# Float32r products that walk their moving rows and their sums from the last column to the first

## The chip, the core and the metric

The kernel runs on one NeuronCore of one Trainium2 chip. TensorE multiplies: it holds a block of weights (128 rows by up to 128 columns) and streams the columns of a moving operand from SBUF through it, adding the results into a PSUM bank of 512 float32 values per partition. VectorE (DVE), ScalarE (ACT) and GpSimd (POOL) do elementwise work, and SyncE (SP) issues most of the DMAs. The metric is the device time of one execution in microseconds, smaller is better. The kernel before takes 1236.33 us, the median of three runs (1235.86 to 1240.36).

## The reference

Two decoder layers over 512 tokens of width 1024, in float32. The mixer of layer 0 is a grouped state-space layer, that of layer 1 attention with forget gates; each is followed by a gated feed-forward block with a short causal convolution. The products with full weight matrices carry most of the arithmetic:

```
for i in range(2):
    hn = rmsnorm(h) * g * (1 + scale) + shift
    m  = s5_mixer(hn) if i == 0 else fox_mixer(hn)     # w_in, w_glu, w_out: 1024 x 1024 / w_in: 1024 x 3088, w_out
    h  = h + gate * m
    hn = rmsnorm(h) * g2 * (1 + scale2) + shift2
    a, b = split(hn @ w_up)                            # 1024 x 5632
    a  = conv_b + sum_j shift_right(a, 2 - j) * conv_w[j]
    h  = h + gate2 * ((silu(a) * b) @ w_down)          # 2816 x 1024
return rmsnorm(h) * final_g
```

The shifts, scales and gates come from a product of silu(c) with a matrix of 1024 x 3072 for each of the four sub-layers.

## The kernel before

**Layout.** Activations lie transposed: features on the 128 partitions (8 tiles of 128 for width 1024), the 512 tokens along the free axis. A weight matrix is cut into tiles of 128 x 128; a tile is the stationary operand and 512 (or 256) tokens of an activation are the moving one. One group of products, over all k tiles of the contraction, fills one PSUM tile of 128 x 512 (or 128 x 256) float32.

**Three products for one.** The operands are float32r, a float32 of reduced precision that TensorE takes in one pass. To keep the accuracy, each operand is split into a high and a low part: ACT writes the high part (`put_parts`, L277) and VectorE the difference (L278). Then high x high, high x low and low x high are added into the same sums. `mms` (L290 to L296) issues these three for one k tile: L294 is the line of nearly every float32r product of the gate and output projections of layer 0, of the query, key and output projections of layer 1, and of the feed-forward blocks where they are computed plainly. `product` (L298) calls it for all tiles: a first part (`head`), in halves of 256 tokens or over all 512; a middle part over all 512 tokens; and a last part (`tail`), always in halves of 256, so that the next norm can begin on the first half.

**Quarters.** In the feed-forward's up projection most pairs of output tiles go through `quarters` (L510), which computes a product of 2 x 2 blocks with seven block products instead of eight. `times` (L546 to L553) issues one block product: 4 k tiles, three parts each, over 256 tokens, 84 products for a pair of tiles, all at L550. The sums are copied or added by ACT (L557) and VectorE (L518).

**The gate of layer 0.** The first four tiles of the gate projection are computed while the state-space part still runs, in `glu_head` (L1189 to L1200, products at L1198, over 512 tokens), first with the high and then with the low parts of the weights.

**What is not float32r or not touched.** The state-space input projection (L1139, L1169) uses plain float32 over 512 tokens. The attention's value projection (L1361) has the activations as stationary operand and 256 (or 272) columns of the weights as moving ones, in float32r; logits (L1470) and weighted values (L1520) are float32r as well.

**Order.** Apart from the start, which is scheduled by hand, the order within each engine follows the program with a few instructions held behind others. TensorE runs its products in that order; semaphores tie it to ACT and VectorE, which split weights ahead of it and empty its sums behind it. Weights are loaded by SP's queue, three raw tiles ahead, and the split parts have five buffers.

Of the kernel before, what the change touches and what calls it, by code (L numbers as in the profile page):

```python
# [19 lines left out]
KT = D // P  # L20
# [46 lines left out]
def part_of(pool, shape, name, tag, bufs, aside=0):  # L67

    _, n, w = shape
    t = pool.tile([P, ROOM if bufs == WB else n * w + P], F32R, name=name, tag=tag, bufs=bufs)  # L70
    return t[:, aside:aside + n * w].rearrange("p (n w) -> p n w", w=w)


class Trunk:
# [215 lines left out]
    def mms(self, o, wk, x, k, nk, cols):  # L290
        (hi, lo) = wk[k]
        xhi, xlo = x(k) if callable(x) else (t[:, k] for t in x)
        for n, (wt, xt) in enumerate(((hi, xhi), (hi, xlo), (lo, xhi))):
            self.last_mm = self.nc.tensor.matmul(  # L294
                o, wt, xt[:, cols], start=(k == 0 and n == 0), stop=(k == nk - 1 and n == 2),
            )  # L296

    def product(self, w, ms, nk, x, evac, head=0, tail=0, after=None, ticks=0, halves=HALVES, tail_pool=(), first=None, step=None):  # L298
# [211 lines left out]
    def quarters(self, pool, l, f, x, finish):  # L510

        nc = self.nc
        H, N = KT // 2, S // 2
        t1, t2 = HALVES
        a, b = (self.raw([P, KT, P], self.io["w_up"][l][2 * f + j]) for j in range(2))
        a11, a12, a21, a22 = a[:, :H], a[:, H:], b[:, :H], b[:, H:]
        c, d = (pool.tile([P, 2, H, P], F32, name="sums", bufs=2) for _ in range(2))
        sub = lambda o, u, v, op=ALU.subtract: nc.vector.tensor_tensor(o, u, v, op)  # L518
        w = {}
        copied = self.copied  # L520

        def parts(src, names, *where):
            hi, lo = (
                pool.tile([P, H * P + P], F32R, name=n, tag="e" + n)[:, ASIDE:ASIDE + H * P].rearrange("p (n w) -> p n w", w=P)
                if where else part_of(self.wpool, [P, len(names) * H, P], n, n, WB, ASIDE)
                for n in ("w_hi", "w_lo")
            )
            with self.behind(*copied):
                self.put_parts(hi, lo, src)
            for j, n in enumerate(names):  # L530
                w[n] = hi[:, j * H:(j + 1) * H], lo[:, j * H:(j + 1) * H]

        parts(a, ("a11", "a12"))
        sub(c[:, 0], a21, a22, ALU.add)
        sub(c[:, 1], c[:, 0], a11)
        parts(c.rearrange("p n k m -> p (n k) m"), ("s1", "s2"))
        sub(d[:, 1], a11, a21)
        sub(d[:, 0], a12, c[:, 1])
        parts(d.rearrange("p n k m -> p (n k) m"), ("s4", "s3"))
        parts(a22, ("a22",), pool)  # L540
        quarter = lambda k, t: tuple(v[:, k * H:(k + 1) * H, t] for v in x)
        xs = {"b11": quarter(0, t1), "b21": quarter(1, t1), "b22": quarter(1, t2)}
        for n, v in self.tx.items():
            xs[f"t{n}"] = v

        def times(o, wn, xn, first=True):  # L546
            (whi, wlo), (xhi, xlo) = w[wn], xs[xn]
            for k in range(H):
                for n, (wt, xt) in enumerate(((whi, xhi), (whi, xlo), (wlo, xhi))):
                    self.last_mm = nc.tensor.matmul(  # L550
                        o, wt[:, k], xt[:, k], start=(first and k == 0 and n == 0), stop=(k == H - 1 and n == 2),
                        skip_group_check=True,
                    )  # L553

        def copy(o, last=False):
            t = self.tmp.tile([P, N], F32, name="nm_h", bufs=4)
            a = nc.scalar.activation(t, o, AF.Copy)  # L557
            if last:
                self.copied = [a.ins]
            return t  # L560

        p1, p5 = (self.mm.tile([P, S], F32, name="mmp")[:, :N] for _ in range(2))
        p2, p4 = (self.aux.tile([P, S], F32, name="aux")[:, :N] for _ in range(2))
        oa, ob = (self.tmp.tile([P, S], F32, name="nm_t") for _ in range(2))
        times(p1, "a11", "b11")
        c1 = copy(p1)
        times(p5, "s1", "t1")
        c5 = copy(p5)
        times(p2, "a12", "b21")
        sub(oa[:, t1], p2, c1, ALU.add)  # L570
        times(p1, "s2", "t2", False)
        c2 = copy(p1, True)
        times(p5, "s4", "b22", False)
        sub(oa[:, t2], p5, c2, ALU.add)
        finish(2 * f, oa, slice(0, S))
        times(p4, "a22", "t4")
        c4 = copy(p4)
        times(p1, "s3", "t3", False)
        sub(ob[:, t2], p1, c5, ALU.add)
        sub(ob[:, t1], p1, c4)  # L580
        finish(2 * f + 1, ob, slice(0, S))
# [98 lines left out]
class Ew:  # L680
# [29 lines left out]
    def sub(self, a, b, out=None):  # L710
        return self.tt(a, b, ALU.subtract, out)
# [70 lines left out]
class S5(Trunk):  # L782
# [292 lines left out]
    def s5(self, i, nxt):  # L1075
# [5 lines left out]
        with ExitStack() as stack:  # L1081
# [7 lines left out]
            with ExitStack() as start:  # L1089
# [11 lines left out]
                with tc.manual_schedule(engines={ENG.PE, ENG.Activation, ENG.DVE, ENG.SP}):  # L1101
# [53 lines left out]
                    first = self.tmp.tile([P, L, B], F32, name="uf", tag="nm_t")  # L1155
# [22 lines left out]
            yhi = ylo = None  # L1178
            raw, hi, lo, gps = {}, {}, {}, {}
# [9 lines left out]
            def glu_head(k, part):  # L1189

                for m in range(HEAD):
                    if part and m not in lo:
                        lo[m] = part_of(self.wpool, [P, KT, P], "w_lo", "w_lo", WB)
                        with tc.issue_after(self.scanned):
                            nc.vector.tensor_tensor(lo[m], raw[m], hi[m].bitcast(F32), ALU.subtract)
                    wt = (hi, lo)[part][m][:, k]
                    for xt in (yhi, ylo) if part == 0 else (yhi,):
                        nc.tensor.matmul(  # L1198
                            gps[m], wt, xt[:, k], start=(k == 0 and part == 0 and xt is yhi), stop=(k == KT - 1 and part == 1)
                        )  # L1200

            ps = self.aux.tile([KT, P], F32, name="aux")
# [9 lines left out]
            for m in range(KT):  # L1212
# [22 lines left out]
                if m == KT - 2:  # L1235
                    yhi = self.act.tile([P, KT, S], F32R, name="a_hi")
# [6 lines left out]
            for k in range(KT - 1):  # L1243
                if k == KT - 2:
                    parts(k)
                glu_head(k, 0)
            for k in range(KT - 1):
                glu_head(k, 1)
# [4 lines left out]
            for p in range(2):  # L1253
                glu_head(KT - 1, p)
# [386 lines left out]
```

## Time and profile before

One execution on the chip was profiled. The table gives what matters of it; busy time is the time in which an engine had at least one instruction running.

| | us |
|---|---|
| median of the runs (lowest, highest) | 1236.33 (1235.86, 1240.36) |
| the profiled execution, its own time | 1233.09 |
| its span, first to last instruction | 1231.3 |
| TensorE products | 1200.5 |
| TensorE weight loads | 1031.2 |
| VectorE | 1009.0 |
| ScalarE | 606.3 |
| GpSimd | 82.7 |

How to read it: each instruction has a start and a length, and its line in the kernel. The ends of products on TensorE are modelled and products overlap, so the length that a row shows for one product is longer than the distance between the starts of two that follow each other; where a rate matters, starts are compared. The chain that ended last is followed back from the last instruction, at each step to the work that released it. In the names of groups, `mmp` and `aux` are the PSUM tiles, `a_hi` and `a_lo` the parts of the normed activations, `ghi` and `glo` those of the gated values, `zhi` and `zlo` those of the gate's output in layer 0, `v` those of the attention's output, `w_hi` and `w_lo` those of weights or of the block sums in `quarters`. An engine's idle time is put down to what ended it.

### The profile page before, as it was taken

How to read it: one execution, taken by the hardware profiler on the slowest of the kernel's cores; microseconds unless marked ns; L12 is line 12 of the kernel's file. 1: busy time of each engine (PE TensorE's matmuls, PEld its weight loads, DVE VectorE, ACT ScalarE, POOL GpSimd, SP SyncE). 2: the span in 40 equal slices, each digit the busy share in tenths (PEclk: the TensorE clock that was granted, in tenths of full speed). 3: DMA queues.
4: the chain of work that ended last, by engine and by line, in shares of the span. 5: the costliest groups of instructions: out<-in, count | busy, mean ns of one | idle time of the engine just before them, and what ended most of it. 6: DMA issues, size and time to landing. Idle time of an engine off the chain costs nothing.

```text
span 1231.3 us, 20566 instructions
## 1 busy us (share of the span) xinstructions
PE 1200.5 (97%) x7921; PEld 1031.2 (84%) x7921; DVE 1009.0 (82%) x1872; ACT 606.3 (49%) x1137; POOL 82.7 (7%) x143
## 2 busy tenths in 40 slices
PE   7999999999999999999999999999999999999997
PEld 2466678898989899889899887878989999999987
DVE  7988886779899988799687578876899887888865
ACT  3543465335544543445443565664366554545443
POOL 0000000100000000000000243430000000000000
PEclk9999999999999999999999999999999999999999
DMA  9776668530354544444445543432122332323231
GB/s 356 244 237 215 223 225 286 192 129 35 129 178 158 192 161 160 152 168 132 125 139 190 176 150 124 147 118 94 70 69 95 120 122 77 116 86 123 95 96 69
DMA packets 74385, 183.83 MB, mean 149 GB/s; under 512 B 23231, under 2 KB 25631, under 8 KB 73263
## 3 DMA queue, kind: packets, MB, share of 16 engines
q1 hardware_dynamic: 68239, 161.02, 38.4%
q0 software_dynamic: 5760, 20.97, 5.0%
q8 instruction: 62, 1.02, 0.3%
q10 hardware_dynamic: 288, 0.52, 0.1%
q14 instruction: 36, 0.29, 0.1%
HBM read 175.57 MB, written 6.92 MB: 148 GB/s over the span
## 4 chain that ended last, share of the span: by engine, by line
PE 75%; DVE 15%; DMA 4%; issue 3%; ACT 2%; POOL 0%; SPq 0%; DVEq 0%; ACTq 0%; POOLq 0%
PE mmp L294 32%; PE mmp L550 16%; PE aux L550 6%; DVE w_lo L278 5%; PE mmp L1169 4%; PE mmp L1361 2%; DMA rawd<-in_w_down 2%; PE aux L971 2%; PE mmp L1198 2%; PE aux L1060 1%; PE aux L1500 1%; PE mmp L205 1%; PE aux L1052 1%; DVE ada_raw L247 1%; PE mmp L1109 1%
## 5 line engine op out<-in xcount | busy, mean ns | idle before, releaser
L278 DVE TENSOR_TENSOR w_lo<-raw,w_hi 128x1024 fp32r<-128x1024 f32 (+4 forms) x173 | 183.3, 1065 | 35.4 <-ACT w_hi L277 34.8
L277 ACT ACTIVATE w_hi<-raw 128x1024 fp32r<-128x1024 f32 (+4 forms) x173 | 154.8, 905 | 101.5 <-PE mmp L294 53.1
L294 PE MATMUL mmp<-ghi,w_hi 128*128 128x512 f32 (+1 forms) x392 | 145.1, 370 | 0.0
L294 PE MATMUL mmp<-glo,w_hi 128*128 128x512 f32 (+1 forms) x392 | 144.8, 369 | 0.0
L294 PE MATMUL mmp<-ghi,w_lo 128*128 128x512 f32 (+1 forms) x392 | 144.5, 369 | 0.0
L294 PE MATMUL mmp<-a_hi,w_hi 128*128 128x512 f32 (+1 forms) x376 | 138.8, 372 | 1.5 <-ACT a_hi L433 1.5
L294 PE MATMUL mmp<-a_hi,w_lo 128*128 128x512 f32 (+1 forms) x376 | 136.6, 364 | 0.3 <-DVE w_lo L278 0.3
L294 PE MATMUL mmp<-a_lo,w_hi 128*128 128x512 f32 (+1 forms) x376 | 136.2, 363 | 0.0
L550 PE MATMUL mmp<-w_hi 128*128 128x256 f32 x396 | 111.4, 281 | 2.6 <-ACT nm_h L557 2.6
L550 PE MATMUL mmp<-w_hi,w_lo 128*128 128x256 f32 x396 | 111.1, 281 | 0.7 <-DVE w_lo L278 0.7
L550 PE MATMUL mmp<-w_lo,w_hi 128*128 128x256 f32 x396 | 111.1, 281 | 0.0
L557 ACT ACTIVATE nm_h<-mmp 128x256 f32<-128x256 f32 x99 | 37.9, 384 | 131.5 <-PE mmp L550 131.5
L278 DVE TENSOR_TENSOR w_lo<-sums,w_hi 128x1024 fp32r<-128x1024 f32 x74 | 90.1, 1219 | 0.3 <-ACT w_hi L277 0.2
L294 PEld LDWEIGHTS mmp<-ghi,w_lo 128*128 128x128 f32 x392 | 74.2, 189 | 12.7 <-DVE w_lo L278 0.4
L294 PEld LDWEIGHTS mmp<-glo,w_hi 128*128 128x128 f32 x392 | 74.5, 190 | 11.1
L277 ACT ACTIVATE w_hi<-sums 128x1024 fp32r<-128x1024 f32 x74 | 76.7, 1054 | 14.4 <-DVE sums L518 11.2
L294 PEld LDWEIGHTS mmp<-ghi,w_hi 128*128 128x128 f32 x392 | 74.2, 189 | 11.4
L294 PEld LDWEIGHTS mmp<-a_hi,w_hi 128*128 128x128 f32 x376 | 70.6, 189 | 13.8 <-issue 2.6
L294 PEld LDWEIGHTS mmp<-a_hi,w_lo 128*128 128x128 f32 x376 | 70.9, 189 | 12.3 <-DVE w_lo L278 1.3
L362 DVE SCALAR_TENSOR_TENSOR h<-mmp,par,h 128x512 f32<-128x512 f32 (+1 forms) x100 | 68.1, 683 | 15.3 <-PE mmp L294 15.0
L294 PEld LDWEIGHTS mmp<-a_lo,w_hi 128*128 128x128 f32 x376 | 71.1, 189 | 9.7
L550 PEld LDWEIGHTS mmp<-w_hi 128*128 128x128 f32 x396 | 74.3, 188 | 3.0 <-ACT nm_h L557 3.0
(317 smaller groups left out, 3092.6 us busy)
## 6 DMA issues: line engine op xcount, KB each, us to landing
raw<-in_w_up SPq DMA_DIRECT2D x88, 512.0 KB, 3.3
raw<-in_ada_w SPq DMA_DIRECT2D x40, 512.0 KB, 6.3
ada_raw<-in_ada_t POOLq DMA_DIRECT2D x40, 512.0 KB, 3.9
nf<-nfd SPq DMA_DIRECT2D x8, 1152.0 KB, 6.5
raw<-in_fox_qk SPq DMA_DIRECT2D x16, 512.0 KB, 3.6
raw<-in_w_down SPq DMA_DIRECT2D x24, 320.0 KB, 3.0
rawd<-in_w_down SPq DMA_DIRECT2D x24, 256.0 KB, 3.4
raw<-in_w_down SPq DMA_DIRECT2D x16, 384.0 KB, 3.3
```

The lines of the kernel that those rows point to most:

```text
L205: self.last_mm = nc.tensor.matmul(ps[32 * qq:32 * qq + 32, :], self.sc32[:, k, :], w[:, q * S:(q + 1) * S], start=(step is steps[0]), stop ...
L247: nc.vector.tensor_tensor_reduce(w, w, self.c_row, 1.0, 0.0, ALU.mult, ALU.add, sums[:, j:j + 1])
L277: nc.scalar.activation(hi, src, AF.Copy)
L278: return nc.vector.tensor_tensor(lo, src, hi.bitcast(F32), ALU.subtract)
L294: self.last_mm = self.nc.tensor.matmul(o, wt, xt[:, cols], start=(k == 0 and n == 0), stop=(k == nk - 1 and n == 2),)
L362: add = self.nc.vector.scalar_tensor_tensor(self.h[:, m, cols], ps, self.par[i][:, 16 + m:17 + m], self.h[:, m, cols], op0=ALU.mult, op1=A ...
L550: self.last_mm = nc.tensor.matmul(o, wt[:, k], xt[:, k], start=(first and k == 0 and n == 0), stop=(k == H - 1 and n == 2), skip_group_che ...
L557: a = nc.scalar.activation(t, o, AF.Copy)
L971: nc.tensor.matmul(ps[g2][:, j, cols], x[rows, a + j, r].rearrange("p c j -> p (c j)"), self.rr[rows, planes, q, :], start=(j == 0 and r = ...
L1169: nc.tensor.matmul(ps, w[m][:, k, :], x[:, k], start=(k == 0), stop=(k == KT - 1))
L1198: nc.tensor.matmul(gps[m], wt, xt[:, k], start=(k == 0 and part == 0 and xt is yhi), stop=(k == KT - 1 and part == 1))
L1361: self.last_mm = nc.tensor.matmul(ps[q, b][:, :n], xt[:, k, tb], wt, start=(k == 0 and i == 0), stop=(k == KT - 1 and i == 2),)
```

## The change

Three lines issue the same products with both patterns reversed. The moving operand is read from its last column to its first, and the sums are written from the last column of the PSUM tile to the first, so each column's sum lands where it did. The stationary operand, the order of the products, their number and their flags (which clears, which adds) stay as they were.

```diff
@@ mms @@
         for n, (wt, xt) in enumerate(((hi, xhi), (hi, xlo), (lo, xhi))):
             self.last_mm = self.nc.tensor.matmul(
-                o, wt, xt[:, cols], start=(k == 0 and n == 0), stop=(k == nk - 1 and n == 2),
+                o[:, ::-1], wt, xt[:, cols][:, ::-1], start=(k == 0 and n == 0), stop=(k == nk - 1 and n == 2),
             )
@@ quarters, times @@
                     self.last_mm = nc.tensor.matmul(
-                        o, wt[:, k], xt[:, k], start=(first and k == 0 and n == 0), stop=(k == H - 1 and n == 2),
+                        o[:, ::-1], wt[:, k], xt[:, k, ::-1], start=(first and k == 0 and n == 0), stop=(k == H - 1 and n == 2),
                         skip_group_check=True,
                     )
@@ s5, glu_head @@
                         nc.tensor.matmul(
-                            gps[m], wt, xt[:, k], start=(k == 0 and part == 0 and xt is yhi), stop=(k == KT - 1 and part == 1)
+                            gps[m][:, ::-1], wt, xt[:, k, ::-1], start=(k == 0 and part == 0 and xt is yhi), stop=(k == KT - 1 and part == 1)
                         )
```

## The prediction

> **What bounds the kernel now.** I read the totals first, then the chain of work that ended last, then TensorE's share line by line, then its start times one after another.
>
> ```profile
> span 1231.3 us, 20566 instructions
> ...
> PE 1200.5 (97%) x7921; PEld 1031.2 (84%) x7921; DVE 1009.0 (82%) x1872; ACT 606.3 (49%) x1137; POOL 82.7 (7%) x143
> ...
> PEclk9999999999999999999999999999999999999999
> ...
> PE 75%; DVE 15%; DMA 4%; issue 3%; ACT 2%; POOL 0%; SPq 0%; DVEq 0%; ACTq 0%; POOLq 0%
> ```
>
> TensorE (PE) is busy for 1200.5 us of a span of 1231.3 us, at a full granted clock in every slice; 75% of the chain is its work. VectorE, the next, has 18% of slack over the whole. So what one product costs on TensorE is what the kernel costs, and a saving on another engine would be worth little.
>
> The change touches three lines. Their rows for the whole span (length of the stretch, TensorE busy with the count of products, weight loads busy with their count):
>
> ```profile
> 0.00:1232.00 1232.00, 584.49 (x2808) 473.72 (x2808) 1.00 0.44 149
> ...
> 0.00:1232.00 1232.00, 332.68 (x2772) 330.71 (x2772) 1.00 0.44 149
> ...
> 0.00:1232.00 1232.00, 22.65 (x96) 17.80 (x96) 1.00 0.44 149
> ```
>
> These are L294, L550 and L1198: 5,676 products, 939.8 us of TensorE's 1200.5. Next, how many of them are 512 columns wide, from the groups kept apart by shape:
>
> ```profile
> L294 PE MATMUL mmp<-ghi,w_hi 128*128 128x512 f32 x312 | 121.8, 390 | 0.0
> L550 PE MATMUL mmp<-w_hi 128*128 128x256 f32 x396 | 111.4, 281 | 2.6 <-ACT nm_h L557 2.6
> ...
> L294 PE MATMUL mmp<-a_hi,w_hi 128*128 128x512 f32 x280 | 111.9, 400 | 0.0
> ...
> L294 PE MATMUL mmp<-v,w_hi 128*128 128x512 f32 x96 | 30.2, 396 | 1.1 <-DVE lo L278 1.1
> ...
> L294 PE MATMUL mmp<-v,w_lo 128*128 128x512 f32 x48 | 18.7, 390 | 0.0
> L294 PE MATMUL mmp<-zhi,w_hi 128*128 128x512 f32 x48 | 18.7, 389 | 0.0
> ...
> L294 PE MATMUL aux<-a_hi,w_hi 128*128 128x512 f32 x8 | 3.1, 389 | 0.0
> ```
>
> Each product comes in three parts of equal count (v's two high parts share one name, hence 96 and 48). So L294 has 3 x (312 + 280 + 48 + 8) + 96 + 48 = 2,088 products of 512 columns and 2,808 - 2,088 = 720 of 256. L1198 adds 96 of 512, and all of L550 (84 for each of 33 pairs of tiles) are of 256. Together: **2,184 products of 512 columns and 3,492 of 256.**
>
> The 389 and 281 ns of these rows are no cost: ends are modelled and products overlap. The cost is the distance of starts. From the order of time (start, length, work):
>
> ```profile
> 417.03 0.39 PE L294 MATMUL mmp<-a_hi,w_hi 128*128 128x512 f32 x1
> ...
> 427.91 0.39 PE L294 MATMUL mmp<-ghi,w_hi 128*128 128x512 f32 x1
> ...
> 433.35 0.28 PE L550 MATMUL mmp<-a_hi,w_hi 128*128 128x256 f32 x1
> ...
> 436.18 0.28 PE L550 MATMUL aux<-a_hi,w_hi 128*128 128x256 f32 x1
> ...
> 664.06 0.28 PE L1361 MATMUL mmp<-w_lo,a_hi 128*128 128x256 f32 x1
> ...
> 671.77 0.28 PE L1361 MATMUL mmp<-w_hi,a_hi 128*128 128x256 f32 x1
> ...
> 128.12 4.56 PE L1169 MATMUL mmp<-a_x,raw 128*128 128x512 f32 x10
> 132.61 0.64 PE L205 MATMUL mmp<-raw,s_sc 128*32 128x512 f32 x4
> ```
>
> Between the first two rows lie 48 starts: 10.88 us / 48 = 226.7 ns for 512 columns. Between the next two lie 24: 2.83 / 24 = 117.9 ns for 256. L1361, float32r too but not touched, has 68 starts in 7.71 us: 113.4 ns for 256, exactly half of 226.7. So the time of a float32r product is its streaming, 0.443 ns a column, and L550 pays 4.5 ns more a product on top. The last two rows give a third price: ten products of plain float32 and 512 columns take 4.49 us, 449 ns each, twice the streaming.
>
> **The change, part by part.** No instruction, DMA, wait or buffer is added, removed or moved. Each of the 5,676 products starts at its last column and steps by minus one, on the moving side and on the side of the sum; the same bytes are read and written, and weights are loaded as before. So all that can change is the time of one product. The profile shows no product with a negative step in its innermost run, so this is an unknown that has to be bounded.
>
> *Low end: nothing.* What other engines show of odd patterns (times are min/median/max):
>
> ```profile
> L1042 DVE TENSOR_TENSOR ua<-ua,ub x8: 684/688/692, 69.0 to 179.4; 128x512 f32<-128x512 f32 x8
> ...
> L1039 DVE TENSOR_TENSOR ua<-m,s_rot x8: 683/688/693, 67.4 to 178.0; 128x512 f32<-128x512 f32 x8
> ...
> L1171 ACT ACTIVATE uf<-mmp x7: 597/598/637, 48.2 to 150.0; 128x512 f32<-128x512 f32 x7
> ...
> L212 ACT ACTIVATE ada_rows<-mmp x4: 597/598/599, 22.4 to 167.6; 128x512 f32<-128x512 f32 x4
> ...
> L1186 ACT ACTIVATE a_hi<-yt x8: 1122/1177/1239, 150.4 to 191.2; 128x512 fp32r<-128x512 f32 x8
> ...
> L277 ACT ACTIVATE zhi<-nm_t x8: 630/634/637, 198.8 to 223.6; 128x512 fp32r<-128x512 f32 x8
> ```
>
> L1042 takes its two halves in reverse (an outer step of minus 256) and costs what L1039 costs, 688 ns. L1171 reads sums from PSUM at a step of 8 elements for the same 598 ns as L212's plain read. Only L1186, which writes SBUF at a step of 8, pays: 1177 against 634 ns. A walk backwards stays among neighbours, so these rows leave a price of nothing open. [...]
>
> ```profile
> L277 ACT ACTIVATE w_hi<-raw 128x1024 fp32r<-128x1024 f32 x97 | 101.9, 1056 | 68.5 <-PE mmp L294 43.5 <-PE mmp L1361 7.7 <-DMA raw<-in_w_up 7.6
> ...
> L277 ACT ACTIVATE w_hi<-raw 128x512 fp32r<-128x512 f32 x33 | 20.6, 625 | 11.4 <-DMA raw<-in_w_up 8.0 <-PE aux L550 2.9 <-ACT w_hi L277 0.5
> ```
>
> (1056 - 625) / 512 = 0.84 ns an element. TensorE takes a column in 0.443 ns, reading one 4-byte element per partition and adding another into PSUM: almost exactly two in ACT's time for one. [...]
>
> *High end.* [...] The nearest row of TensorE is L1169's: 449 ns for 512 columns. Farther up stands L1186's price, 1177 - 634 = 543 ns more for 512 elements.
>
> **I take the lost pair**, at the row of the same engine, shape and element size: 449 ns for 512 columns, half of it for 256. Sum: 2,184 x (449 - 226.7) ns = 485 us, plus 3,492 x (224.5 - 117.9) ns = 372 us: 857 us more. Some of it fills time in which TensorE now waits: 1231.3 - 1200.5 = 30.8 us of idle, and 584.5 - (2,088 x 0.2267 + 720 x 0.1179) = 26.3 us in L294 and 332.7 - 2,772 x 0.1179 = 5.9 us in L550 of products that follow one another late. Of these 63 us I give back 20, because part lies where nothing changes (before 168 us, and in the attention's own products) and part is the tail of a product ahead of a wait. VectorE's 1009 us and ACT's 606 us then lie well inside. The profiled execution's own time is 1233.1 us (span 1231.3 and 1.8 around it), 0.3% under the median of 1236.3 us; 1233 + 857 - 20 = **2,070 us**. Its own range: 2,010 us, if all 63 us are filled and L1169's 449 ns has some 2% of changes between groups in it, to 2,125 us, if nothing is filled and streaming doubles exactly (2,184 x 227 + 3,492 x 113 ns = 890 us).
>
> [...]
>
> **The rivals.**
> [...]
> *A smaller price.* The backward walk costs at its start only, for instance L550's 4.5 ns once more on each product (5,676 x 4.5 = 26 us, 1,260 us), or a quarter of the streaming (0.25 x (2,184 x 226.7 + 3,492 x 113.4 ns) = 223 us, 1,456 us). For it: L550's 4.5 ns show that something besides the columns counts. Against it: nothing in the trace makes it depend on direction.
> *Overlap lost.* A product waits until the one before has ended: the 389 and 281 ns of the groups instead of 226.7 and 117.9. That is 2,184 x 162 + 3,492 x 163 ns = 923 us, less 20: 2,136 us. The 256-column distance tells it from the lost pair, 281 against 225.
> *Every element by itself*, at L1186's price: 2,184 x 543 + 3,492 x 271 ns = 2,132 us more, about 3,350 us. Against it: L1186 steps by eight elements.
> *Faster.* L550's extra 4.5 ns go because weights and moving rows, read at the same time, then meet less often: (2,772 + 720) x 4.5 ns = 16 us, 1,217 us. For it: L1361 runs without them. Against it: nothing says that direction is the reason.
>
> **How the numbers follow.** Lost pair 0.46, no price 0.20, smaller price 0.13, overlap lost 0.06, every element 0.07, faster 0.08. Predicted: 2,070 us, the likeliest. The range of 1,230 to 2,140 us takes in lost pair, no price, smaller price and overlap lost, 0.85; it is wide because the two main cases lie 830 us apart. What a measurement of this kernel can tell from no change is about 0.5%. Faster 0.08, same 0.20, slower 0.72.
>
> **What the changed profile would show.** Right: starts of L294's 512-column products 430 to 455 ns apart, of L550's 215 to 232, while L1169 stays at 449 and L1361, whose products stay forward, at 113; VectorE's and ACT's busy times unchanged and their shares down to half and 30%; the chain over 85% TensorE; the granted clock full. A clock below full would spoil the comparison of distances. Wrong at the pair: distances of 227 and 118. Wrong at the overlap: 389 and 281. Wrong in what is given back: distances as said but a time outside 2,010 to 2,125 us. If only one of the two sides, reading or adding, is to blame, this one profile can't say which.

## The result, and the profile after

The changed kernel takes 1244.38 us, the median of 13 runs (1240.75 to 1252.66), against 1235.86 us of the kernel before (13 runs, 1230.60 to 1243.71). The ratio is 1.0078, with a 95% interval of 1.0057 to 1.0098: slower by 8.5 us by the two medians and by some 9.6 by the ratio, where 834 us more had been predicted. The way was right, the size was not.

The totals, the granted clock and the chain of waits of the kernel after (its profiled execution took 1242.51 us):

```profile
span 1240.7 us, 20613 instructions
...
PE 1214.0 (98%) x7921; PEld 1034.2 (83%) x7921; DVE 1007.4 (81%) x1872; ACT 606.2 (49%) x1137; POOL 82.6 (7%) x143
...
PEclk9999999999999999999999999999999999999999
...
PE 82%; DVE 11%; DMA 3%; ACT 2%; issue 2%; DVEq 0%; SPq 0%; ACTq 0%
```

The span grew by 1240.7 - 1231.3 = 9.4 us. TensorE's busy time grew by 1214.0 - 1200.5 = 13.5 us, and its idle time fell from 30.8 to 26.7 us, which gives 4.1 us back. VectorE and ACT work as long as before.

The three lines of the change, over the whole span (L294, L550, L1198; columns as in the prediction, and the third number from the end is the mean granted clock):

```profile
0.00:1242.00 1242.00, 596.92 (x2808) 475.47 (x2808) 0.99 0.45 148
...
0.00:1242.00 1242.00, 332.97 (x2772) 331.38 (x2772) 0.99 0.45 148
...
0.00:1242.00 1242.00, 23.19 (x96) 17.74 (x96) 0.99 0.45 148
```

L294 takes 12.4 us more and L1198 0.5; L550, all of 256 columns, 0.3. So the price sits in the products of 512 columns. The same products in order of time as those that the prediction showed (start, length, work):

```profile
419.42 0.40 PE L294 MATMUL mmp<-a_hi,w_hi 128*128 128x512 f32 x1
...
430.62 0.40 PE L294 MATMUL mmp<-ghi,w_hi 128*128 128x512 f32 x1
...
436.22 0.28 PE L550 MATMUL mmp<-a_hi,w_hi 128*128 128x256 f32 x1
...
439.05 0.28 PE L550 MATMUL aux<-a_hi,w_hi 128*128 128x256 f32 x1
...
670.02 0.28 PE L1361 MATMUL mmp<-w_lo,a_hi 128*128 128x256 f32 x1
...
677.73 0.28 PE L1361 MATMUL mmp<-w_hi,a_hi 128*128 128x256 f32 x1
```

The 48 starts of 512 columns now take 11.20 us instead of 10.88: 233.3 ns each, 6.7 more. The 24 of 256 columns take 2.83 us as before, 117.9 ns in the mean, though no longer evenly: by the starts in the trace they come 115, 118 and 120 ns apart in turns. L1361, which stayed forward, is at 113.4. From the distances, 2,184 x 6.67 ns = 14.6 us; L294 and L1198 show 13.0, because some late starts got shorter (by the trace, the time by which 512s start late fell from 6.6 to 3.9 us).

### The profile page after: what moved, and what is told of

It reads as the page before. It is cut to its first block, busy times and chain, and to the rows that moved or that the text cites. A ratio compares the mean times of both kernels' runs of the same rounds, so it can differ in the third digit from the quotient of the medians.

```text
span 1240.7 us, 20613 instructions
## 1 busy us (share of the span) xinstructions
PE 1214.0 (98%) x7921; PEld 1034.2 (83%) x7921; DVE 1007.4 (81%) x1872; ACT 606.2 (49%) x1137; POOL 82.6 (7%) x143
## 4 chain that ended last, share of the span: by engine, by line
PE 82%; DVE 11%; DMA 3%; ACT 2%; issue 2%; DVEq 0%; SPq 0%; ACTq 0%
PE mmp L294 39%; PE mmp L550 16%; PE aux L550 6%; PE mmp L1169 4%; DVE w_lo L278 3%; PE mmp L1361 2%; PE aux L971 2%; DMA rawd<-in_w_down 1%; PE aux L1500 1%; PE mmp L1198 1%; PE mmp L205 1%; PE aux L1060 1%; PE aux L1052 1%; PE mmp L1109 1%; PE aux L1470 1%
## 5 line engine op out<-in xcount | busy, mean ns | idle before, releaser
L294 PE MATMUL mmp<-ghi,w_hi 128*128 128x512 f32 (+1 forms) x392 | 147.9, 377 | 0.0
L294 PE MATMUL mmp<-glo,w_hi 128*128 128x512 f32 (+1 forms) x392 | 147.6, 376 | 0.0
L294 PE MATMUL mmp<-ghi,w_lo 128*128 128x512 f32 (+1 forms) x392 | 147.6, 376 | 0.0
L294 PE MATMUL mmp<-a_hi,w_hi 128*128 128x512 f32 (+1 forms) x376 | 140.7, 377 | 1.5 <-ACT a_hi L433 1.5
L294 PE MATMUL mmp<-a_hi,w_lo 128*128 128x512 f32 (+1 forms) x376 | 138.2, 368 | 0.0
L294 PE MATMUL mmp<-a_lo,w_hi 128*128 128x512 f32 (+1 forms) x376 | 138.2, 368 | 0.0
L550 PE MATMUL mmp<-w_hi 128*128 128x256 f32 x396 | 110.9, 280 | 1.7 <-ACT nm_h L557 1.7
L550 PE MATMUL mmp<-w_hi,w_lo 128*128 128x256 f32 x396 | 111.6, 282 | 0.5 <-DVE w_lo L278 0.5
L550 PE MATMUL mmp<-w_lo,w_hi 128*128 128x256 f32 x396 | 111.5, 282 | 0.0
L294 PEld LDWEIGHTS mmp<-ghi,w_lo 128*128 128x128 f32 x392 | 74.7, 191 | 14.1
L294 PEld LDWEIGHTS mmp<-glo,w_hi 128*128 128x128 f32 x392 | 74.9, 191 | 12.9
L294 PEld LDWEIGHTS mmp<-ghi,w_hi 128*128 128x128 f32 x392 | 74.8, 191 | 12.7
L294 PEld LDWEIGHTS mmp<-a_hi,w_hi 128*128 128x128 f32 x376 | 70.3, 188 | 15.2 <-issue 2.6
L294 PEld LDWEIGHTS mmp<-a_hi,w_lo 128*128 128x128 f32 x376 | 70.7, 188 | 12.8
L294 PEld LDWEIGHTS mmp<-a_lo,w_hi 128*128 128x128 f32 x376 | 70.8, 188 | 10.9
L550 PEld LDWEIGHTS mmp<-w_hi 128*128 128x128 f32 x396 | 74.4, 188 | 1.9 <-ACT nm_h L557 1.9
```

Of the source, the lines that this page charges most:

```text
L294: self.last_mm = self.nc.tensor.matmul(o[:, ::-1], wt, xt[:, cols][:, ::-1], start=(k == 0 and n == 0), stop=(k == nk - 1 and n == 2),)
L550: self.last_mm = nc.tensor.matmul(o[:, ::-1], wt[:, k], xt[:, k, ::-1], start=(first and k == 0 and n == 0), stop=(k == H - 1 and n == 2), ...
```

## The experiments

All ratios are against the kernel before on the same chip, with 95% intervals. The first four runs were to tell three theories apart. A: the reading of the moving rows meets the loading of the next weights. B: adding into PSUM in falling order has a price. C: every column read backwards costs 0.013 ns more, hidden in products of 256 by the weight load.

**Only the reading reversed** (e1_read), at all three lines; the columns of the sums come out mirrored.

```diff
-                o, wt, xt[:, cols], ...
+                o, wt, xt[:, cols][:, ::-1], ...
-                        o, wt[:, k], xt[:, k], ...
+                        o, wt[:, k], xt[:, k, ::-1], ...
-                            gps[m], wt, xt[:, k], ...
+                            gps[m], wt, xt[:, k, ::-1], ...
```

> All 5,676 products read their moving rows from the last column, but write their sums in rising order (the sums land mirrored in the tokens, so the values are not the reference's). Theory A (the reading meets the loading of the next weights, which starts 4 ns after each product): the whole price is here. Starts of 512-column products 233.4 ns apart as in the changed kernel, 256-column ones at 115 to 120 in turns, ratio to before 1.006 to 1.009. Theory B (the price is that of adding into PSUM in falling order): distances of 226.7 and 117.9 as before, ratio 0.998 to 1.002. Theory C (each column read backwards costs 0.013 ns more, hidden in 256-column products by the weight load): as A.

**Only the sums reversed** (e2_sum), mirrored likewise.

```diff
-                o, wt, xt[:, cols], ...
+                o[:, ::-1], wt, xt[:, cols], ...
-                        o, wt[:, k], xt[:, k], ...
+                        o[:, ::-1], wt[:, k], xt[:, k], ...
-                            gps[m], wt, xt[:, k], ...
+                            gps[m][:, ::-1], wt, xt[:, k], ...
```

> All 5,676 products read in rising order and write their sums from the last column (sums mirrored, values not the reference's). A and C: nothing changes, 226.7 and 117.9 ns, ratio 0.998 to 1.002. B: the whole price, 233.4 ns for 512 columns, ratio 1.006 to 1.009. If both sides pay, 512 columns lie between 228 and 232 ns here and in the run with reading alone.

The same 48 starts of 512 columns, first with the reading reversed, then with the sums reversed:

```profile
424.90 0.40 PE L294 MATMUL mmp<-a_hi,w_hi 128*128 128x512 f32 x1
...
436.10 0.40 PE L294 MATMUL mmp<-ghi,w_hi 128*128 128x512 f32 x1
```

```profile
416.44 0.39 PE L294 MATMUL mmp<-a_hi,w_hi 128*128 128x512 f32 x1
...
427.32 0.39 PE L294 MATMUL mmp<-ghi,w_hi 128*128 128x512 f32 x1
```

11.20 us or 233.3 ns with the reading reversed, 10.88 us or 226.7 ns with the sums reversed. The times agree: e1_read 1246.35 us, ratio 1.0068 (1.0041 to 1.0095), the whole effect; e2_sum 1237.75 us, ratio 0.9995 (0.9969 to 1.0021), none. B falls. The 47 additional instructions of the changed kernel are there in e2_sum too (20,613) and not in e1_read (20,566); they are semaphore instructions that come with the reversed sums (50 more on TensorE's queue and 3 fewer on VectorE's), and cost nothing that can be measured.

**Only the products of 512 columns reversed** (e3_wide), both sides; L1198 is as in the change, L550 and the halves of L294 run forward.

```diff
-                o, wt, xt[:, cols], ...
+                (o[:, ::-1] if cols.stop - cols.start == S else o), wt, (xt[:, cols][:, ::-1] if cols.stop - cols.start == S else xt[:, cols]), ...
```

> Both patterns reversed, but only in the 2,184 products of 512 columns; the 3,492 of 256 columns stay forward. A, B and C: 512 columns at 233.4 ns, 256 back at an even 118, ratio 1.006 to 1.009, the whole of the change. If the 256-column products contributed through stalls, a third or more of the 0.8% would be missing here (ratio under 1.005).

```profile
420.90 0.40 PE L294 MATMUL mmp<-a_hi,w_hi 128*128 128x512 f32 x1
...
432.11 0.40 PE L294 MATMUL mmp<-ghi,w_hi 128*128 128x512 f32 x1
...
437.70 0.28 PE L550 MATMUL mmp<-a_hi,w_hi 128*128 128x256 f32 x1
437.82 0.28 PE L550 MATMUL mmp<-a_lo,w_hi 128*128 128x256 f32 x1
...
440.45 0.28 PE L550 MATMUL aux<-a_hi,w_hi 128*128 128x256 f32 x1
```

The 512s are at 11.21 us / 48 = 233.5 ns, as every theory expected. No theory had what the 256s do: forward, as in the kernel before, but 24 starts in 2.75 us, 114.6 ns. By the trace the first four are 118 to 120 ns apart and nearly all that follow 113 or 114, in 30 of the 31 stretches of L550 to the end or nearly so. L550's busy time fell from 332.7 to 322.4 us. That pays for the reversed 512s: 1236.08 us, ratio 0.9988 (0.9965 to 1.0012). So the time of a product doesn't hang on its own direction alone.

**TensorE alone** (e4_alone): settings of 20 products, one after another, with nothing else running; nothing of the reference is computed.

> Products alone, no other engine at work: 20 float32r products in a row for each setting (the kernel computes nothing of the reference and returns x). Settings: 512, 384, 320 and 256 columns with neither, one or both sides reversed; weights moved by 4 to 112 elements against the moving rows, forward and reading backward; stationary operands of 64 columns. A: the price is a stall per product that comes from the weight load: the same 6 to 7 ns at 384 and 320 columns as at 512, it changes with the offset of the weights, and with 64-column weights (a shorter load) it is about half. B: it shows with the sums alone reversed. C: it grows with the columns (5 ns at 384, 4 at 320), does not depend on the offset of the weights, and 256-column products with 64-column weights show 3 to 4 ns of it.

Distances of starts in ns (mean of the last 17; reading and adding forward or reversed, weights at shift 0):

```
columns             512     384     320     256
both forward      226.7   173.5   146.7   119.8
reading reversed  233.2   177.5   146.5   118.2
sums reversed     226.7   174.9   146.8   119.7
both reversed     233.2   177.6   146.5   118.2
```

The reading sets the price (the sums alone show one at 384 columns only, 1.4 ns), and it isn't proportional: 6.6 ns at 512 columns, 4 at 384, none at 320, and 1.6 less at 256. C falls; A's figure for 384 and 320 was missed as well, and so was A's half price with weights of 64 columns (reversed 512s 233.2 ns still; forward 256s 113.4, reversed 117.7). The shifts of the weights were tried again behind a fixed prelude (e9_meet, below).

**Does a pace carry over?** Theory S: a run of products keeps a pace that the products before it left it with; forward 256s have two steady ones, 118 and 113.4 ns. Rival P: every product has its own price, and they add up. Rival W: the 113.4 ns needs whole reversed stretches. First, **only the 256s reversed** (e5_narrow; L1198 runs forward):

```diff
-                o, wt, xt[:, cols], ...
+                (o if cols.stop - cols.start == S else o[:, ::-1]), wt, (xt[:, cols] if cols.stop - cols.start == S else xt[:, cols][:, ::-1]), ...
-                        o, wt[:, k], xt[:, k], ...
+                        o[:, ::-1], wt[:, k], xt[:, k, ::-1], ...
```

> Only the 3,492 products of 256 columns are reversed; those of 512 run forward. Theory S (a run of float32r products keeps a pace that the products before it left it with: forward 256s have two steady paces, 118 and 113.4 ns, and reversed ones cannot hold the faster): 256s at 115/118/120 in turns, mean 118, nowhere 113; 512s back at 226.7 ns; ratio 0.998 to 1.002. Rival P (every product has its own price and prices add up: the whole change less its 512-column half): the changed kernel's 1.008 less the 0.999 of the 512s alone, so 1.009, with the 256s some 3 ns dearer than before.

```profile
438.66 0.28 PE L550 MATMUL mmp<-a_hi,w_hi 128*128 128x256 f32 x1
...
441.49 0.28 PE L550 MATMUL aux<-a_hi,w_hi 128*128 128x256 f32 x1
```

2.83 us for 24 starts, 117.9 ns, nowhere a steady 113; the 512s are at 226.7. 1241.58 us, ratio 1.0025 (1.0001 to 1.0049): a little over S's range, far from P's 1.009. The halves don't add up to the whole, because in the whole the reversed 512s can't bring the reversed 256s to 113 (e8_history, below).

**Three reversed products, then one, at the end of every full-width group** (e6_last3, e7_last1; everything else forward):

```diff
-                o, wt, xt[:, cols], ...
+                (o[:, ::-1] if k == nk - 1 and cols.stop - cols.start == S else o), wt, (xt[:, cols][:, ::-1] if k == nk - 1 and cols.stop - cols.start == S else xt[:, cols]), ...
```

In e7_last1 the condition has `n == 2` as well.

> All forward but the last k tile (three products) of every full-width group of mms; each such group leads into a run of 256s or into another group. Theory S: three reversed products are enough to leave the next 256s at 113.4 ns in place of 118 (in the run with all 512s reversed the new pace was reached within four 256s): L550 from 332.7 to about 322 us, L294 about 2 us up, ratio 0.989 to 0.994. Rival W (the 113.4 ns came from whole reversed stretches, or from something else in that kernel): 256s stay at 118, ratio 1.000 to 1.003.

> As the kernel with three, but only the very last product of every full-width group is reversed. Theory S leaves open how many it takes: if one is enough, ratio 0.988 to 0.993 and 256s at 113.4 ns; if not, 256s at 118 and ratio 1.000 to 1.002. Rival W: 1.000 to 1.002.

L550 in e7_last1, in order of time and over the span, then its totals:

```profile
436.27 0.28 PE L550 MATMUL mmp<-a_hi,w_hi 128*128 128x256 f32 x1
...
438.99 0.28 PE L550 MATMUL aux<-a_hi,w_hi 128*128 128x256 f32 x1
```

```profile
0.00:1242.00 1242.00, 321.96 (x2772) 319.94 (x2772) 0.99 0.45 148
```

```profile
span 1232.0 us, 20583 instructions
...
PE 1198.1 (97%) x7921; PEld 1025.2 (83%) x7921; DVE 1008.2 (82%) x1872; ACT 606.2 (49%) x1137; POOL 83.9 (7%) x143
```

One reversed product ahead of a stretch is enough: 24 starts in 2.72 us, 113.3 ns, 30 of the 31 stretches end at 113, and 10.7 us are off L550's busy time. The times are 1231.07 us and 0.9959 (0.9932 to 0.9987) for e6_last3, 1232.92 us and 0.9954 (0.9931 to 0.9977) for e7_last1, against 1237.04 before: both are faster than the kernel before and the changed one. W falls. Single executions spread by 1%, and the one profiled here (1233.82 us) lay above its kernel's median where that of the kernel before (1233.09) lay below, so the ratio counts and not these spans. The gain is some 5 us and not the 9 to 15 of S's range. In this execution TensorE's clock was half for 20.5 us, against 6.8 us in the one of the kernel before: 58 of the 159 products of the three lines that are followed over 12 ns (256 columns) or 33 ns (512) late lie there, against 13 of 112 before, and they make most of the 5.9 us by which L294 and L1198 are busier. Besides, TensorE's idle time is 1232.0 - 1198.1 = 33.9 us (30.8 before). What the clock does to the times is taken up at the end of this section.

**What sets the pace, with TensorE alone** (e8_history): forward 256s, with the kernel's addresses, after different preludes.

> TensorE alone, addresses and the order high x high, high x low, low x high as in the kernel; it computes nothing of the reference. Runs of 40 products of 256 columns after different preludes, each prelude twice. Theory S: after 24 forward 512s the forward 256s run at 118 ns to their end, after 24 reversed ones at 113.4; somewhere between 1 and 12 reversed 512s at the end of the prelude the pace changes from one to the other; reversed 256s run at a mean of 118 after either; a wait of TensorE at the hand-over can change the pace too, as the two stalls in the kernel before did. Rival W or P: the same pace after every prelude.

The 20th and the 40th of four runs of 40, after 24 forward 512s; after 24 reversed; after 24 forward and two reversed; after 24 forward and three reversed:

```profile
40.56 0.28 PE L68 MATMUL zaab<-xb,wa 128*128 128x256 f32 x1
...
42.92 0.28 PE L68 MATMUL zaab<-xa,wa 128*128 128x256 f32 x1
...
50.82 0.28 PE L68 MATMUL zabb<-xb,wa 128*128 128x256 f32 x1
...
53.09 0.28 PE L68 MATMUL zabb<-xa,wa 128*128 128x256 f32 x1
...
71.70 0.28 PE L68 MATMUL zadc<-xb,wa 128*128 128x256 f32 x1
...
73.97 0.28 PE L68 MATMUL zadc<-xa,wa 128*128 128x256 f32 x1
...
82.50 0.28 PE L68 MATMUL zaec<-xb,wa 128*128 128x256 f32 x1
...
84.85 0.28 PE L68 MATMUL zaec<-xa,wa 128*128 128x256 f32 x1
```

20 starts in 2.36, 2.27, 2.27 and 2.35 us: 118, 113.5, 113.5 and 117.5 ns, all the same forward products at the same addresses. S holds, but the dose is no threshold: behind 24 forward 512s, one reversed 512 leaves 117.8 ns, two 113.4, three 117.8, six and twelve 113.4, and three with one forward 512 behind them 113.4 again. One reversed 256 gives 113.3, three 117.8, six 113.3. A wait of TensorE brought 117.8 after either prelude, and reversed 256s ran at 117.9 after either. Every prelude came twice, with the same pace both times.

**One reversed 256 ahead of each pair** (e10_first), 33 products in all:

```diff
-                        o, wt[:, k], xt[:, k], ...
+                        (o[:, ::-1] if wn == "a11" and k == 0 and n == 0 else o), wt[:, k], (xt[:, k, ::-1] if wn == "a11" and k == 0 and n == 0 else xt[:, k]), ...
```

> All forward but one product of 256 columns: the first of each of the 33 pairs in quarters; 33 products of 5,676. By theory S, and by the run of TensorE alone where one reversed 256 after forward 512s left the next 256s at 113.4 ns: L550 from 332.7 to about 321 us with starts 113/114 apart from the third product on, L294 as before at 584 to 588 us, ratio 0.990 to 0.997; where three pairs follow one another the second or third may fall back to 118. By the rival that the pace hangs on reversed 512s, or that the kernel's other engines give all of it back: 256s at 118, or the ratio within 0.2% of 1.

A miss: 432.18 to 435.00 us for the 24 starts shown of the other kernels, 117.5 ns, and 1236.81 us, ratio 0.9990 (0.9966 to 1.0013). The dose that worked with TensorE alone doesn't in the kernel, as one or three reversed 512s worked in the kernel and not alone. That a pace carries over is shown; which dose sets it has to be tried in place.

**What meets what** (e9_meet). Rival I to theory A: walking backwards has its own price, whatever the weights.

> TensorE alone; it computes nothing of the reference. After the same 24 forward 512s (two reversed ones behind them for one set of 256s), 30 products each with the weights' first column shifted by 0 to 96 elements, the moving rows shifted by 0, 16 or 32, or with 96 to 16 columns of weights in place of 128. Theory A (the moving rows' read meets the loading of the next weights): forward 512s leave 226.7 ns for up to 234 at some shifts of the weights, and come back to it where the moving rows are shifted as far; reversed ones stay at 233 or above at full width and come down as the weights get narrower, to 220 to 227 at 16 columns. Rival I (walking backward has its own price, whatever the weights): forward 226.7 and reversed 233.3 at every shift and every width. For 256s by A the forward pace splits in two by prelude at some shifts only and falls to 113 or below for both directions with narrow weights; by I it does not depend on the shift.

Mean distances in ns over the last 20 starts, by the shift of the weights in elements:

```
weights' shift    0      4      8      16     24     32     48     64     96
512 forward     226.7  226.7  233.4  233.4  234.4  232.4  229.1  226.7  232.4
512 reversed    233.4  233.4  233.4  233.4  233.4  236.7  233.3  233.3  236.7

columns of weights at shift 0   128    96     64     32     16
512 forward                   226.7  230.1  230.1  231.7  231.4
512 reversed                  233.4  233.4  233.3  233.4  233.3
```

The 10th and the 30th product, reversed at shift 0; forward at shift 16; forward with the weights and the moving rows both shifted by 16; reversed with 16 columns of weights:

```profile
56.35 0.40 PE L68 MATMUL zabc<-xa,wa 128*128 128x512 f32 x1
...
61.02 0.40 PE L68 MATMUL zabc<-xa,wb 128*128 128x512 f32 x1
...
118.45 0.39 PE L68 MATMUL zagc<-xa,wa 128*128 128x512 f32 x1
...
123.11 0.39 PE L68 MATMUL zagc<-xa,wb 128*128 128x512 f32 x1
...
292.72 0.39 PE L68 MATMUL zauc<-xa,wa 128*128 128x512 f32 x1
...
297.26 0.39 PE L68 MATMUL zauc<-xa,wb 128*128 128x512 f32 x1
...
454.03 0.40 PE L68 MATMUL zbhc<-xa,wa 128*16 128x512 f32 x1
...
458.69 0.40 PE L68 MATMUL zbhc<-xa,wb 128*16 128x512 f32 x1
```

Forward products pay the same 233 ns (4.66 us / 20) when the weights lie 8 or 16 elements off, and are back at 227 (4.54 us / 20) when the moving rows are moved as far; with both moved by 32 they are at 226.7. So forward has a cheap place, at which the kernel before happens to sit, and reversed has none among these shifts, nor among the 20 of e4_alone (233.2 to 236.6). Here A is right and I wrong. In the width I is right and A wrong: with 16 columns of weights in place of 128 nothing comes off the reversed price (4.66 us / 20). Of the 256s, at full width, the pace depended on the prelude clearly at a shift of 16, the kernel's (117.9 and 113.3 ns), by 0.4 to 1.2 ns at 8, 32 and 96, and not at 0, 48 or 64 (120.0, 117.8 and 120.0); reversed they never went below 117.6, narrow weights or not, where A had expected 113 with narrow ones.

**The same in the kernel.** Weights of L294 16 elements later, nothing reversed (e11_aside); the same on top of the whole change (e12_both):

```diff
-    def weights(self, w, nk, *pool, aside=0):
+    def weights(self, w, nk, *pool, aside=ASIDE):
```

> Nothing is reversed. The weights of all products of mms lie 16 elements later in their buffers, as those of the last halves and of quarters do already; so most 512-column products meet their moving rows at a shift of 16 in place of 0. Theory A (the price of the change is a lost alignment between the moving rows' addresses and the weights'): as in the run of TensorE alone at that shift, 512s go from 226.7 to 233 ns and L294 from 584 to 592 to 598 us, although every product runs forward; the ratio is 1.004 to 1.010 if L550 stays at 118 ns and 0.994 to 1.000 if it falls to 113.4 as behind reversed 512s. Theory I (only walking backward costs): 512s stay at 226.7 ns, ratio 0.998 to 1.002.

> The whole change, and the weights 16 elements later as well. Theory A: the alignment is lost already, so the two prices do not add up: 512s at 233.3 ns, 256s at 115/118/120 in turns, ratio 1.005 to 1.010 like the change alone. Theory I, or two prices of their own: the change's 6.7 ns and whatever the shift costs by itself add up, so if the shifted forward kernel has 233 ns, this one has about 240 ns and a ratio of 1.014 to 1.02.

```profile
420.43 0.39 PE L294 MATMUL mmp<-a_hi,w_hi 128*128 128x512 f32 x1
...
431.63 0.39 PE L294 MATMUL mmp<-ghi,w_hi 128*128 128x512 f32 x1
...
437.23 0.28 PE L550 MATMUL mmp<-a_hi,w_hi 128*128 128x256 f32 x1
...
439.96 0.28 PE L550 MATMUL aux<-a_hi,w_hi 128*128 128x256 f32 x1
```

```profile
427.91 0.40 PE L294 MATMUL mmp<-a_hi,w_hi 128*128 128x512 f32 x1
...
439.11 0.40 PE L294 MATMUL mmp<-ghi,w_hi 128*128 128x512 f32 x1
```

With nothing reversed the 48 starts take 11.20 us, 233.3 ns, as in the changed kernel, and behind them the 256s fall to 2.73 us / 24 = 113.8 ns, as in e3_wide; the ratio is 0.9996 (0.9972 to 1.0021). With both, again 11.20 us: the two do not add up to 240 ns. 1242.77 us, ratio 1.0040 (1.0015 to 1.0064), a little under the range expected and overlapping the change alone. I falls: forward products pay 233.3 ns as well, and the two prices do not add up. A's part on the addresses holds in the kernel. That reversed reads pay for the same meeting with the weights is argued from the equal price and the missing sum, and the width (e9_meet) speaks against it; no run reads backwards without a load of weights beside it.

**The granted clock behind the small differences.** TensorE's clock is full but for stretches of 3.4 us, or a few of them in a row, in which it is half: 6.8 us in all in the profiled execution of the kernel before, 10.2 in that of the changed one. One such stretch of e1_read and one of e7_last1 (third number from the end: granted clock), each with two of its 512-column products that lie eight starts apart, reversed in e1_read and forward in e7_last1:

```profile
174.92:181.75 6.83, 6.83 (x23) 5.77 (x23) 5.44 (x8) 3.54 (x5) 0.00 (x0) 0.50 0.38 105
...
177.44 0.63 PE L1198 MATMUL mmp<-a_lo,w_hi 128*128 128x512 f32 x1
...
180.86 0.63 PE L1198 MATMUL mmp<-a_lo,w_hi 128*128 128x512 f32 x1
```

```profile
174.69:181.52 6.83, 6.83 (x22) 5.67 (x22) 5.74 (x8) 3.22 (x4) 0.00 (x0) 0.50 0.46 123
...
176.79 0.63 PE L1198 MATMUL mmp<-a_lo,w_hi 128*128 128x512 f32 x1
...
180.21 0.63 PE L1198 MATMUL mmp<-a_lo,w_hi 128*128 128x512 f32 x1
```

Both are 3.42 us / 8 = 427.5 ns: at half the clock the direction costs nothing, and the distance is less than twice 226.7. What brings such stretches was not tried, but the time follows them. Among the 26 executions of the kernel before beside e1_read, the three with a mean clock of 0.987 took 1244.5 to 1246.2 us, the three at 0.996 and 0.997 took 1232.2 to 1234.9. Time multiplied by mean clock, an estimate of the time at full clock, averages 1227.8 to 1228.2 us for the kernel before in each of its four sets of runs, 1236.2 for the change, 1236.7 for e1_read, 1236.0 for e12_both, 1229.0 for e5_narrow and 1221.4 for e7_last1. By it e5_narrow (1.0006) and e12_both (1.0066) lie inside what was expected of them; e7_last1 gains 6.8 us, still short of S's range.

## Why the prediction was wrong

- **What bounds the kernel** was right: TensorE's share went from 97 to 98%, VectorE and ACT kept their busy times, the clock stayed near full (a mean of 0.995 and 0.994). So was the count: 2,184 products of 512 columns carry the loss.
- **"I take the lost pair" is the step that failed.** It put 449 and 224.5 ns; 233.3 and 117.9 were measured. That TensorE moves two neighbouring elements in a step, so that falling order could lose a pair, was the author's supposition, and no run shows it. What the runs show in its place: for the side of the sums no price (e2_sum, 226.7 ns and 0.9995), for the reading 3% of a 512-column product (e1_read, 233.3 against 226.7 ns). L1169's 449 ns, the row it was taken from, belongs to another kind of product, plain float32: in the trace of before that line has 112 rows for the 56 products it issues, where L550 has 2,772 for 2,772, so the ten rows are five products, and 449 ns is half of one. Nor is it a steady pace: eight of the ten distances are 429 or 430 ns, the first 533 and the last 522.
- **The range**, 1,230 to 2,140 us, holds the result only because it takes in the rivals; the main case is 826 us off. Its own low end has a slip: 2% off the 449 ns gives 1,992 us and not 2,010.
- **The low end's reason**, that a walk backwards stays among neighbours (L1042, L1171), was nearer than the high end: 6.7 ns more on a 512-column product, where the high end had 222. It was set back on the same supposition about pairs, and got 0.20.
- **"Of these 63 us I give back 20"** was mis-sized with the rest: of 13.5 us more work, 4.1 were given back.
- **The rivals.** The time came nearest to the smaller price (1,260 us as its low end, from 4.5 ns more on every product), but its form was wrong: 6.7 ns on the 512s and nothing on the 256s. The rival "Faster" had named a cause that fits the forward products (226.7 or 233.4 ns by the shift of the weights, e9_meet), reads at the same time that meet more or less often, and set against it that nothing tied this to direction. Direction does enter, the other way: reversed reads cost 6.7 ns more on 512 columns where the kernel's weights lie (e1_read). Its sum for L550, 2,772 x 4.5 ns = 12.5 us, is nearly what e7_last1 gets from L550 (10.7 us).
- **What the trace of before had shown.** L550 at 117.9 and L1361 at 113.4 ns are products of one kind and size. The starts of L550 itself held both: 4 of its 31 stretches end at 113. A cost that takes two values for the same instruction is a cost of circumstances, and weighs more for a small disturbance than a row of another data type.

TensorE's weight loads begin with the product that runs while they are read: in the trace of after those at L294 start a median of 4 ns behind it and take some 190 ns of the 233 to the next start. Two rows of the kernel after (PEld is the weight load):

```profile
419.42 0.40 PE L294 MATMUL mmp<-a_hi,w_hi 128*128 128x512 f32 x1
419.42 0.19 PEld L294 LDWEIGHTS mmp<-a_lo,w_hi 128*128 128x128 f32 x1
```

That the distance depends on where weights and moving rows lie to each other is shown for forward products (226.7 or 233.4 ns in e9_meet, 233.3 ns in e11_aside). Why reversed ones find no cheap place, which of the two reads waits, and why narrower weights don't make it cheaper, stays open.

## What to carry to other kernels

Before pricing a new access pattern by a row of another kind of instruction, look whether the same instruction already has two prices in the trace; the difference is the likelier size. Back-to-back products have here a pace that depends on the relative addresses of weights and moving rows (226.7 or 233.4 ns for forward 512s, e9_meet) and on what ran just before (113.4 or 117.8 ns for forward 256s, e8_history), so half of a change may show nothing, and halves need not add up. It can be used, but has to be tried in place: reversing the last product of every 512-column group of L294 made this kernel 0.5% faster (0.9954), one reversed 256 ahead of each pair did not (0.9990). And before a difference of some tenths of a percent is explained, look at the granted clock of the executions.

## What was not expected of the hardware

- Float32r products of 512 columns start 226.7 to 236.7 ns apart depending on the weights' address against the moving rows' and on the direction of reading (e9_meet); forward, a shift of 64 elements is as good as none (226.7), one of 16 costs 6.7 ns.
- Forward products of 256 columns have two steady paces at the same addresses, 113.4 and 117.8 ns, chosen by the products before them (e8_history) and kept over 40 products there, and in the kernel to the end of stretches of 84 (113.3 ns in e7_last1).
- Where the granted clock is half, 512s start 427.5 ns apart, forward (e7_last1) and reversed (e1_read) alike: the price of direction shows at full clock only.
- Sums written from the last column to the first cost nothing on 512 columns: 226.7 ns alone in either order (e4_alone), and a ratio of 0.9995 in the kernel (e2_sum).
